# Down projections of a two-layer decoder by 2x2-block products, with block results accumulated in DRAM

## The chip, the cores and the metric

The kernel runs on one core of one Trainium2 chip. A core has five engines with a queue each: PE (matrix products; its weight loads are counted apart as PEld), DVE (vector work), ACT (scalar functions and copies), POOL, and SP, which here only issues transfers. ACT and POOL can issue transfers too. An engine works its queue in order and waits at an instruction until what it needs is done. The time is that of one execution on the device, in microseconds (us); of several runs the median is given.

## The reference

The model is one inference step for 1024 prompt tokens and 8 sample tokens, together T = 1032, with a residual stream of D = 1024 and two layers. Layer 0 mixes tokens by a gated linear recurrence, layer 1 by attention in a window of 128. After each mixer comes the part that is changed here:

```python
def sq_relu_mlp(x, w_up, w_down):
    return jnp.square(jax.nn.relu(x @ w_up)) @ w_down

yp = yp + sq_relu_mlp(rms_norm(yp, norm_mlp_g[layer]), mlp_w_up[layer], mlp_w_down[layer])
ys = ys + sq_relu_mlp(rms_norm(ys, norm_mlp_g[layer]), mlp_w_up[layer], mlp_w_down[layer])
```

The hidden size is 4096: w_up is 1024 x 4096 and w_down 4096 x 1024. Everything is float32.

## The kernel before

Activations lie transposed, as 128 features by the 1032 tokens, so a residual stream is 8 tiles (`x`), a hidden layer 32 (the *k tiles* of the down projection). A float32 factor is split into a high part, rounded to the format that PE takes, and a low part, the rest. A product then takes three passes: high by high, high by low, low by high (L208 and L486). The cast to the high part is ACT's (L150, L370, L376), the subtraction for the low part DVE's (L151, L371, L377).

**Up projection** (`up`, from L497). Its outputs are made in 16 pairs q of two 128-row tiles: he (even) and ho (odd). Each pair, seen as 2x2 blocks with the tokens cut in two halves of 516, is computed with seven block products instead of eight (`BY`, `ORDER`): the factors of a product are sums of blocks. Weight sums S1 to S4 are made by DVE (L462) and split. One product is 24 matmuls of 258 columns (4 k tiles, 3 passes, 2 parts; `product`, L486). Copies by ACT (L519, L524, L527, L534) and adds by DVE (L521, L528, L530, L532) take the results out of PSUM and combine them; then r squared times the squared relu (L537, L538), and ACT issues the store of the tile to `hid` in DRAM (L539).

**Down projection** (`down`, from L566). Here all is done directly: hidden tiles come back from DRAM, loaded by SP (L548) and split (L376, L377). They are taken in groups of 8, 8, 8, 4 and 4. For a group and each of the 8 output tiles, `proj` runs 9 matmuls of 344 columns for each k tile, and DVE adds the three results into the residual tile x, which stays on chip (L591). x is loaded from the buffer `spill` in the first group (L578). The last group goes together with the next norm (`down_steps`, L310). While a group is computed, the next group's tiles are loaded; the first is prepared during the last up pair (`ahead_of_down`).

Weights come through two raw tiles (`raws`, L144), one unit of 128 x 1024 at a time, in the order of one list. Tiles live in pools: W (12 tiles of 128 x 1024) for weights and their sums, A (33 tiles of 128 x 1032) for activations. A pool hands out its tiles in turn, and whoever gets one waits until its last user is done. PSUM is named by banks in turns; in products a block uses G for the result that collects several products, X or Y for those that stand alone. The code gives the operations in program order; a scheduler places them on each engine's queue, with priority for what `tc.high_priority()` encloses and not before the last PSUM copy for what `tc.issue_after(last["copy"])` encloses. After that each queue's order is fixed.

Of the kernel before, what the change touches and what calls it, by code (L numbers as in the profile page):

```python
# [26 lines left out]
HALF = T // 2  # L27
QT = T // 4
# [28 lines left out]
def trunk(ctx: ExitStack, tc: tile.TileContext, I, O):  # L57
# [83 lines left out]
    def fetch(n):  # L141
        while len(raws) < min(n, len(units)):
            raws.append(rp.tile([P, D], F32, tag="R", name=nm("raw")))
            sp.dma_start(raws[-1], units[len(raws) - 1][2])  # L144
# [23 lines left out]
    for layer in range(2):  # L168
        add_units(f"up{layer}", I["w_up"][layer], 2 * NPAIR, lambda j: None)
        add_units(f"dn{layer}", I["w_dn"][layer], 32, lambda j: W)  # L170
# [259 lines left out]
    PROG = [(q, i) for q in (0, 1) for i in (1, 2)] + [(q, i) for i in (3, 7, 6, 5, 4) for q in (0, 1)]  # L430
    PROG += [(q, i) for q in range(2, NPAIR) for i in ORDER]

# [3 lines left out]
    class PairWeights:  # L436
        def __init__(self, layer):
            self.layer = layer
            self.builds = []
            for q in range(NPAIR):  # L440
                names = ["A11", "A12", "+S1", "+S2", "S2", "+S3", "S3", "S1", "+S4", "A22", "S4"]
                if q < 2:
                    names = ["A11", "A12", "+S1", "+S2", "+S3", "+S4", "A22", "S4", "S3", "S2", "S1"]
                self.builds += [(q, n) for n in names]
# [4 lines left out]
        def source(self, q, name):  # L449
            if q not in self.src:  # L450
                n = f"up{self.layer}"
                ensure(index[n, 2 * q + 1])
                x, y = loaded.pop((n, 2 * q)), loaded.pop((n, 2 * q + 1))
                self.src[q] = {"A21": x[:, 0:512], "A11": x[:, 512:1024], "A12": y[:, 0:512], "A22": y[:, 512:1024]}
            src = self.src[q]
            if name not in src:
                x, y, op = SUMS[name]
                x, y = self.source(q, x), self.source(q, y)
                if name in ("S1", "S3"):
                    src[name, 1] = W("ws")  # L460
                src[name] = src[("S1" if name in ("S1", "S2") else "S3"), 1][:, slice(512, 1024) if name in ("S2", "S4") else slice(0, 512)]
# [3 lines left out]
        def build(self, upto):  # L465
            while self.n < min(upto, len(self.builds)):
                q, name = self.builds[self.n]
                if name[0] == "+":
                    self.source(q, name[1:])
                else:  # L470
                    self.ops[q, name] = op_of(self.source(q, name), W, 512)
                self.n += 1

        def take(self, q, name):
            self.build(self.builds.index((q, name)) + 1)
            return self.ops.pop((q, name))

        def look(self, n):
            self.build(self.builds.index((PROG[n][0], BY[PROG[n][1]][0])) + 1 + LOOK)
# [17 lines left out]
    def up(layer, tok, pw, r, hid, after):  # L497
        ops = tok.ops
        st = {}
        for n, (q, i) in enumerate(PROG):  # L500
            w, x = BY[i]
            if n in (1, 3, 5, 7, 9):
# [3 lines left out]
            wt = pw.take(q, w)  # L506
            if i == 1:
                st[q] = {2: DB("X" if q == 1 else "Y"), "g": DB("G"), "e": A("he"), "o": A("ho")}
            z = st[q]
            alone = i in (1, 2, 7) or (i == 3 and q < 2)  # L510
            if alone and i in (3, 7):
                z[i] = DB("Y" if q == 0 else "X")
            d = z["g"] if i in (1, 5, 6) else z[7] if i == 4 else z.get(i, z["g"])
            product(d, alone, wt, ops[x])
            e, o, g = z["e"], z["o"], inner(z["g"])
            e0, e1, o0, o1 = [quarters(t[:, h]) for t in (e, o) for h in (H0, H1)]
            if i == 1:
                with tc.high_priority():
                    last["copy"] = act.copy(e0, g).ins  # L519
            elif i == 2:  # L520
                dve.tensor_tensor(e0, inner(d), e0, ALU.add)  # L521
            elif i == 6:
                with tc.high_priority():
                    last["copy"] = act.copy(o0, g).ins  # L524
            elif i == 5:
                with tc.high_priority():
                    last["copy"] = act.copy(o1, g).ins  # L527
# [5 lines left out]
            elif i == 3:  # L533
                last["copy"] = act.copy(e1, inner(d)).ins  # L534
            ready = {4: [(o, 2 * q + 1)], 3: [] if alone else [(e, 2 * q)], 5: [(e, 2 * q)] if 3 in z else []}
            for t, k in ready.get(i, []):
                dve.scalar_tensor_tensor(t, t, 0.0, r, ALU.min, ALU.mult)  # L537
                act.activation(t, t, AF.Square)  # L538
                act.dma_start(hid[k], t)  # L539
# [750 lines left out]
```

## Time and profile before

| what | us |
|---|---|
| median of 3 runs (2121.7 to 2123.92) | 2121.81 |
| profiled execution | 2123.98 |
| its span | 2122.2 |
| up stage of layer 0, PE without a break (373.60 to 677.00) | 303.40 |
| down stage of layer 0 but its last group (683.66 to 1001.47) | 317.81 |
| up stage of layer 1 (1444.90 to 1748.50) | 303.60 |
| down stage of layer 1 but its last group (1755.20 to 2073.00) | 317.80 |

The profile page gives busy time per engine, the chain of work that ended last, and the costliest groups of instructions by line, with their mean duration and what ended the idle time before them. In a group, "out<-in" names the tiles. "128x516 f32" is 128 partitions by 516 elements. Transfers are listed by the queue that issued them and the median time from issue to landing.

### The profile page before, as it was taken

To read this page: it belongs to the slowest core of one execution; us is meant where nothing else is said; L and a number is where in the kernel's file an instruction comes from. 1 tells how busy PE (TensorE), PEld (TensorE's weight loads), DVE (VectorE), ACT (ScalarE), POOL (GpSimd) and SP (SyncE) were. 2 spreads that over 40 slices of the span, in tenths; PEclk is the share of its full clock that TensorE was granted. 3 is DMA by queue.
4 is the path that set the end of the run, shared out by engine and by line. 5 is a ranking of instruction groups with operands and counts; after the bars stand their busy time and mean duration, and the time that the engine had idled before them with its cause. 6 is when DMAs were issued, how large, how long until landed. Compare 5 with 4: busy or idle time off the path is not lost.

```text
span 2122.2 us, 35371 instructions
## 1 busy us (share of the span) xinstructions
PE 2084.0 (98%) x14518; PEld 2050.3 (97%) x14518; DVE 1193.7 (56%) x2062; ACT 893.8 (42%) x1633; POOL 198.3 (9%) x294
## 2 busy tenths in 40 slices
PE   6999999999999999999999998999999999999999
PEld 5999999999999999999999997999999999999999
DVE  6988547855555432424757878578555545324142
ACT  5486545534444220211447878555434433112010
POOL 4552100000000000000003444000000000000000
PEclk9999999999999999999999999999999999999999
DMA  5102142232234541321232322622323256313112
GB/s 168 50 21 62 51 163 77 99 102 110 90 120 178 202 140 50 120 80 57 94 85 71 96 58 72 230 71 90 110 90 111 100 180 219 139 52 120 50 51 80
DMA packets 84609, 218.05 MB, mean 103 GB/s; under 512 B 15448, under 2 KB 40544, under 8 KB 84448
## 3 DMA queue, kind: packets, MB, share of 16 engines
q1 hardware_dynamic: 64864, 169.29, 24.9%
q10 hardware_dynamic: 19584, 46.51, 5.6%
q8 instruction: 114, 1.87, 0.4%
q14 instruction: 47, 0.39, 0.1%
HBM read 149.83 MB, written 53.24 MB: 96 GB/s over the span
## 4 chain that ended last, share of the span: by engine, by line
PE 91%; DVE 4%; ACT 3%; issue 1%; POOL 1%; DMA 0%; ACTq 0%; SPq 0%; DVEq 0%; POOLq 0%
PE bD L486 31%; PE bP L208 26%; PE bS L208 16%; PE bT L208 8%; PE bP L677 4%; PE bO L805 2%; PE bS L760 1%; PE bT L781 1%; PE bN L623 1%; PE bS L705 1%; DVE xc L1044 1%; DVE t L289 1%; DVE wl L151 0%; DVE hl L236 0%; ACT wh L150 0%
## 5 line engine op out<-in xcount | busy, mean ns | idle before, releaser
L486 PE MATMUL bD<-op,op 128*128 128x258 f32 x5376 | 654.2, 283 | 1.4 <-ACT ho L527 1.4
L486 PEld LDWEIGHTS bD<-op,op 128*128 128x128 f32 x5376 | 648.9, 189 | 6.5 <-ACT ho L527 6.1
L150 ACT CAST wh<-raw 128x1024 fp32r<-128x1024 f32 (+1 forms) x116 | 117.3, 1019 | 429.8 <-PE bP L208 190.3
L208 PE MATMUL bP<-hdl,wh 128*128 128x344 f32 x768 | 191.2, 320 | 0.0
L208 PE MATMUL bP<-hdh,wl 128*128 128x344 f32 x768 | 191.2, 320 | 0.0
L208 PE MATMUL bP<-hdh,wh 128*128 128x344 f32 x768 | 191.0, 320 | 0.0
L151 DVE TENSOR_TENSOR wl<-raw,wh 128x1024 fp32r<-128x1024 f32 (+1 forms) x113 | 135.5, 1202 | 56.8 <-ACT wh L150 51.6
L591 DVE TENSOR_TENSOR x<-bP,x 128x344 f32<-128x344 f32 x96 | 44.9, 509 | 159.7 <-PE bP L208 156.4
L208 PEld LDWEIGHTS bP<-hdh,wl 128*128 128x128 f32 x768 | 134.2, 188 | 0.0
L208 PEld LDWEIGHTS bP<-hdl,wh 128*128 128x128 f32 x768 | 134.1, 188 | 0.0
L208 PEld LDWEIGHTS bP<-hdh,wh 128*128 128x128 f32 x768 | 134.1, 188 | 0.0
L371 DVE TENSOR_TENSOR op<-ws,op 128x512 fp32r<-128x512 f32 x128 | 87.7, 689 | 76.4 <-ACT op L370 76.2
L208 PE MATMUL bS<-hdh,wh 128*128 128x344 f32 x512 | 127.6, 320 | 0.4 <-ACT he L534 0.4
L208 PE MATMUL bS<-hdl,wh 128*128 128x344 f32 x512 | 127.5, 320 | 0.0
L208 PE MATMUL bS<-hdh,wl 128*128 128x344 f32 x512 | 127.4, 320 | 0.0
L377 DVE TENSOR_TENSOR hdl<-hdl,hdh 128x1032 fp32r<-128x1032 f32 x64 | 77.5, 1228 | 63.5 <-ACT hdh L376 63.4
L376 ACT CAST hdh<-hdl 128x1032 fp32r<-128x1032 f32 x64 | 66.4, 1056 | 86.8 <-DMA hdl<-hid 84.6
L370 ACT CAST op<-ws 128x512 fp32r<-128x512 f32 x128 | 78.7, 619 | 50.4 <-PE bD L486 43.8
L371 DVE TENSOR_TENSOR op<-raw,op 128x512 fp32r<-128x512 f32 x96 | 66.1, 691 | 43.1 <-ACT op L370 42.9
L208 PEld LDWEIGHTS bS<-hdh,wh 128*128 128x128 f32 x512 | 89.4, 188 | 0.6 <-ACT he L534 0.6
L208 PEld LDWEIGHTS bS<-hdl,wh 128*128 128x128 f32 x512 | 89.5, 188 | 0.0
L208 PEld LDWEIGHTS bS<-hdh,wl 128*128 128x128 f32 x512 | 89.4, 188 | 0.0
(294 smaller groups left out, 4204.3 us busy)
## 6 DMA issues: line engine op xcount, KB each, us to landing
hdl<-hid SPq DMA_DIRECT2D x64, 516.0 KB, 6.3
raw<-w_up SPq DMA_DIRECT2D x64, 512.0 KB, 3.5
raw<-w_dn SPq DMA_DIRECT2D x64, 512.0 KB, 3.6
hid<-he ACTq DMA_DIRECT2D x32, 516.0 KB, 3.5
hid<-ho ACTq DMA_DIRECT2D x32, 516.0 KB, 2.6
x<-spill SPq DMA_DIRECT2D x24, 516.0 KB, 6.0
spill<-y ACTq DMA_DIRECT2D x48, 172.0 KB, 1.9
raw<-w_in SPq DMA_DIRECT2D x16, 512.0 KB, 3.7
```

The source lines that it names most:

```text
L150: act.copy(r_(hi[:, sl]), raw[:, sl])
L151: eng.tensor_tensor(r_(lo[:, sl]), raw[:, sl], hi[:, sl], ALU.subtract)
L208: pe.matmul(o, lhsT=r_(wt[:, col(k):col(k) + P]), rhs=r_(xt[:, cs(c)]), start=(k == 0 and a == 0), stop=(k == nk - 1 and a == 2))
L289: dve.scalar_tensor_tensor(t, xs[m][:, cs(c)], V(gname, m), r, ALU.mult, ALU.mult)
L370: act.copy(r_(t[:, 0:n]), src)
L371: dve.tensor_tensor(r_(t[:, n:2 * n]), src, t[:, 0:n], ALU.subtract)
L376: act.copy(r_(hi), lo)
L377: dve.tensor_tensor(r_(lo), lo, hi, ALU.subtract)
L486: pe.matmul(d[:, 512 * b:512 * b + QT], lhsT=r_(wt[:, j * P:j * P + P]), rhs=r_(xt[:, QT * b:QT * b + QT]), start=first and j == 0 and a = ...
L591: dve.tensor_tensor(xs[m][:, cs(c)], ps[c], xs[m][:, cs(c)], ALU.add)
L677: pe.matmul(ps[c], lhsT=r_(wt[:, k * P:k * P + P]), rhs=r_(xt[:, cs(c)]), start=(k == 0 and a == 0), stop=(k == M8 - 1 and a == 2))
L805: pe.matmul(o, lhsT=r_(x), rhs=r_(y[:, d]), start=(n == 0), stop=(n == 3 * (2 - first) - 1))
```

## The change

The first 28 of the 32 k tiles of each down projection (14 of 16 pairs, `NSP`) are also computed by seven products of 2x2 blocks. The last four k tiles, in one group with the norm, stay as they were.

- The 14 pairs are cut in five *chunks* (`CHUNKS`) of 3, 3, 3, 3 and 2 pairs. For each chunk there are four output blocks of 2 x 128 rows: 20 blocks per layer. A block is seven products of 18 matmuls of 258 columns (12 in the last chunk, *chunk 4*), in the same loop as the up pairs (`PROG`, `mlp_products`). `PairWeights` makes the weight sums for both; its operations are 384 columns wide (256 in chunk 4) in the down blocks. The weights in DRAM are laid out anew, in 40 units of 768 or 512 columns and 4 of 1024 per layer.
- The right factors are seven sums of quarters of the hidden pair, 516 columns each. They are made once, as an up pair ends (`sums_of`): four DVE operations, and four stores by ACT into `hsum` in DRAM (seven sums, 258 KB each), in place of the two stores of 516 KB. Pairs 14 and 15 are stored in `hid` as before.
- In the down blocks SP loads the sums again (`load`), each chunk's during the chunk before: 8 over the first three blocks, the other 13 (of 21) over the last block, three per product. Four products after a load is issued, the tile is split into high and low by ACT and DVE (`Ahead.split`).
- A block's two results, he and ho, are taken out of PSUM as in the up pairs. They are not added to tiles on chip: POOL issues a transfer for each that adds it to the residual in DRAM (`accum_op=ALU.add`), 80 in all of 516 KB. After a block's accumulates in chunk 4, POOL also issues the loads of the two x tiles (16 in all), and between them the loads of the last four hidden tiles (`last_tile`; 8 in all).

```diff
+CHUNKS = [range(0, 3), range(3, 6), range(6, 9), range(9, 12), range(12, 14)]
+NSP = CHUNKS[-1][-1] + 1
...
+    PROG += [("dn", b, i) for b in range(4 * len(CHUNKS)) for i in ORDER]
...
+    def load(src, n):
+        t = A("tl")
+        sp.dma_start(t[:, n:2 * n], src)
+        return t[:, 0:n], t[:, n:2 * n]
...
+        def fetch(self, c, upto, step):
+            done = 7 * len(CHUNKS[c]) - len(self.left[c])
+            for _ in range(max(0, min(upto - done, len(self.left[c])))):
+                name, p = self.left[c].pop(0)
+                self.raw.append((step, c, name, load(self.sums[p][:, PLACE[name]], HALF)))
+
+        def split(self, step):
+            with tc.issue_after(last["copy"]):
+                while self.raw and self.raw[0][0] <= step - 4:
+                    _, c, name, t = self.raw.pop(0)
+                    self.ops[c][name].append(op_at(*t))
+
+    def sums_of(e, o, to):
+        t = W("ts")
+
+        def put(k, x):
+            act.dma_start(to[:, k * HALF:k * HALF + x.shape[1]], x)
+
+        put(2, o)
+        yield
+        dve.tensor_tensor(t[:, H0], e[:, H1], e[:, H0], ALU.subtract)
+        dve.tensor_tensor(e[:, H1], o[:, H1], e[:, H1], ALU.subtract)
+        dve.tensor_tensor(t[:, H1], o[:, H1], t[:, H0], ALU.subtract)
+        yield
+        put(0, e)
+        put(4, t)
+        dve.tensor_tensor(o[:, H0], o[:, H0], t[:, H1], ALU.subtract)
+        yield
+        put(6, o[:, H0])
...
+        def last_tile(k):
+            lo, hi = A("hdl"), A("hdh")
+            pool.dma_start(lo, hid[layer][k])
+            return hi, lo
...
+            product(d, alone, wt, (tok if up else ahead).ops[x] if up else ahead.ops[q // 4][x])
...
+            if ready and up:
+                t = z[ready]
                 dve.scalar_tensor_tensor(t, t, 0.0, r, ALU.min, ALU.mult)
                 act.activation(t, t, AF.Square)
-                act.dma_start(hid[k], t)
+                if q >= NSP:
+                    act.dma_start(hid[layer][2 * (q - NSP) + (ready == "o")], t)
+            elif ready:
+                pool.dma_start(acc[2 * (q % 4) + (ready == "o")], z[ready], accum_op=ALU.add)
             if i == (4 if 3 in z else 3):
+                if up and q < NSP:
+                    stores.append(sums_of(e, o, hsum[layer][q]))
                 del st[q]
...
+            if up and q == NPAIR - 1:
+                k = ORDER.index(i)
+                ahead.fetch(0, 3 * (k + 1), n)
+                ahead.split(n)
+            elif not up:
+                c, k = q // 4, 7 * (q % 4) + ORDER.index(i)
+                ahead.split(n)
+                if c + 1 < len(CHUNKS):
+                    ahead.fetch(c + 1, 8 * k // 20 if k <= 20 else 8 + len(CHUNKS[c]) * (k - 20), n)
                 else:
+                    if k in (2, 6, 10, 14):
+                        raw.append(last_tile((k - 2) // 4))
+                    if k in (5, 9, 13, 17):
+                        with tc.issue_after(last["copy"]):
+                            hs.append(op_at(*raw.pop()))
+                    if i == 3:
+                        for m in (2 * (q % 4), 2 * (q % 4) + 1):
+                            xs.append(A("x"))
+                            pool.dma_start(xs[m], acc[m])
```

How this moves instructions shows at three places of layer 0. The names in the rows: spill1 is the residual in DRAM, hid0 the hidden tiles, hsum0 the stored sums, raw a raw weight tile, tl a sum, hdl and hdh a hidden tile's low and high part, bD a PSUM bank, op and wh split weights. In brackets stand the counters that a row waits for: DMASW those of transfers issued by POOL, DMAHW of the others. First, before the change, SP's queue in the first group of `down`, where x and the next group's hidden tiles are loaded between weights.

```order
L578 DMA x805_7215<-spill1_2533 128x1032 [waits DMAHW6_49,PE_49]
L548 DMA hdl809_7223<-hid0_2535 128x1032 [waits PE_49]
L144 DMA raw824_7399<-w_dn 128x1024 [waits DMAHW4_49,DMAHW0_49,DVE_49]
L144 DMA raw833_7490<-w_dn 128x1024 [waits DMAHW5_49,DMAHW1_49,DVE_49]
L578 DMA x814_7306<-spill1_2533 128x1032 [waits DMAHW2_49,PE_49]
L548 DMA hdl818_7314<-hid0_2535 128x1032 [waits DMAHW3_49,PE_49]
L578 DMA x823_7397<-spill1_2533 128x1032 [waits PE_49,Pool_49]
L548 DMA hdl827_7405<-hid0_2535 128x1032 [waits PE_49]
```

These rows are gone from SP. The changed kernel's POOL queue in chunk 4; before, POOL issued no transfer. Block 16 has ho1141 and he1140, block 17 ho1163 and he1162.

```order
L613 DMA spill1_2533<-ho1141_10221 128x1032 [waits DMASW2_49,DVE_49]
L613 DMA spill1_2533<-he1140_10220 128x1032 [waits DMASW3_49,Activation_49]
L641 DMA x1158_10355<-spill1_2533 128x1032 [waits DMASW4_49,DMASW3_49,PE_49]
L641 DMA x1159_10357<-spill1_2533 128x1032 [waits DMAHW0_49,DMAHW2_49,DMASW2_49,PE_49]
L571 DMA hdl1171_10435<-hid0_2535 128x1032 [waits DMAHW6_49,DMAHW7_49,DMASW6_49,PE_49]
L613 DMA spill1_2533<-ho1163_10362 128x1032 [waits DMASW7_49,DVE_49]
L613 DMA spill1_2533<-he1162_10361 128x1032 [waits DMASW0_49,Activation_49]
L641 DMA x1178_10495<-spill1_2533 128x1032 [waits DMASW1_49,DMASW0_49,PE_49]
L641 DMA x1179_10497<-spill1_2533 128x1032 [waits DMASW7_49,PE_49]
L571 DMA hdl1185_10519<-hid0_2535 128x1032 [waits DMAHW6_49,PE_49]
```

The loads of x and of the last hidden tiles have moved from SP to POOL and stand behind the accumulates: x1158 waits for both accumulates of its block, and hdl1171 stands behind it.

Second, ACT's queue before, towards the end of `down`, where it only splits weights and hidden tiles.

```order
L150 CAST wh932_8564<-raw923_8473 128x1024 [waits DMAHW3_49,DVE_49,PE_49]
L150 CAST wh940_8653<-raw931_8562 128x1024 [waits DMAHW4_49,DVE_49,PE_49]
L376 CAST hdh895_8124<-hdl894_8123 128x1032 [waits DMAHW7_49,PE_49]
L376 CAST hdh903_8213<-hdl902_8212 128x1032 [waits DMAHW6_49,PE_49]
L376 CAST hdh911_8302<-hdl910_8301 128x1032 [waits DMAHW0_49,PE_49]
L150 CAST wh948_8742<-raw939_8651 128x1024 [waits DMAHW5_49,DVE_49,PE_49]
L376 CAST hdh919_8391<-hdl918_8390 128x1032 [waits DMAHW1_49]
L376 CAST hdh927_8480<-hdl926_8479 128x1032 [waits DMAHW2_49]
```

No row there reads PSUM. ACT's queue in the changed kernel at blocks 17 (he1162) and 18 (he1182, ho1183).

```order
L596 COPY he1162_10361<-bD1161_10360 128x516 [waits PE_49]
L382 CAST hdh1172_10436<-hdl1171_10435 128x1032 [waits DMASW6_49]
L376 CAST op1207_10688<-ws1197_10616 128x256
L376 CAST op1209_10705<-raw1193_10592 128x256 [waits PE_49]
L376 CAST op1210_10708<-ws1205_10670 128x256 [waits DVE_49]
L153 CAST wh1214_10763<-raw1194_10594 128x1024 [waits DMAHW1_49,PE_49]
L596 COPY he1182_10501<-bD1181_10500 128x516
L596 COPY ho1183_10502<-bD1181_10500 128x516 [waits PE_49]
L153 CAST wh1217_10769<-raw1213_10761 128x1024 [waits DMAHW2_49]
L382 CAST hdh1186_10520<-hdl1185_10519 128x1032 [waits DMASW3_49]
L596 COPY ho1183_10502<-bD1181_10500 128x516 [waits PE_49]
```

PSUM copies (L596), which PE waits for, now stand in the same queue behind casts that wait for POOL's loads: hdh1172 ahead of the copies of block 18, hdh1186 ahead of the second copy into ho1183.

Third, SP's queue in the changed kernel in the last block of chunk 1, where the sums of chunk 2 are loaded (L515) beside weights (L147); before, the down stage held the rows of the first place here.

```order
L515 DMA tl945_8481<-hsum0_2537 128x516 [waits DMASW1_49]
L147 DMA raw969_8629<-w_dn 128x768 [waits DMAHW5_49,DMAHW2_49,DVE_49]
L147 DMA raw970_8631<-w_dn 128x768 [waits DMAHW3_49,DMAHW6_49,DVE_49,Activation_49]
L515 DMA tl951_8509<-hsum0_2537 128x516 [waits DMAHW4_49,DMASW3_49]
L515 DMA tl952_8511<-hsum0_2537 128x516 [waits PE_49]
L515 DMA tl953_8513<-hsum0_2537 128x516 [waits PE_49]
L515 DMA tl955_8538<-hsum0_2537 128x516 [waits DMAHW7_49,PE_49]
L515 DMA tl956_8540<-hsum0_2537 128x516 [waits DMAHW0_49,PE_49]
L515 DMA tl957_8542<-hsum0_2537 128x516 [waits DMAHW1_49,PE_49]
L515 DMA tl960_8570<-hsum0_2537 128x516 [waits DMAHW2_49,PE_49]
L515 DMA tl961_8572<-hsum0_2537 128x516 [waits DMAHW3_49,PE_49]
L515 DMA tl962_8574<-hsum0_2537 128x516 [waits DMAHW4_49,DMASW5_49,Activation_49]
```

Ten loads of 258 KB stand nearly without a break, two of them waiting for accumulates (DMASW3, DMASW5) of earlier blocks.

170 lines of the change are left out of this document (75 added, 95 removed).

## Prediction

> **What bounds the kernel now.** I read the shares by engine and the chain first, then busy time by stretch, then the groups of the two MLP stages with their durations, last the DMA issues. The stretches are, in order, layer 0's up and down projections and layer 1's; the columns are length, busy time of PE, PEld, DVE, ACT and POOL (with instruction counts), granted TensorE clock, DMA share and GB/s.
>
> ```profile
> PE 2084.0 (98%) x14518; PEld 2050.3 (97%) x14518; DVE 1193.7 (56%) x2062; ACT 893.8 (42%) x1633; POOL 198.3 (9%) x294
> PE bD L486 31%; PE bP L208 26%; PE bS L208 16%; PE bT L208 8%; PE bP L677 4%; PE bO L805 2%; PE bS L760 1%; PE bT L781 1%; PE bN L623 1%; PE bS L705 1%; DVE xc L1044 1%; DVE t L289 1%; DVE wl L151 0%; DVE hl L236 0%; ACT wh L150 0%
> 373.60:677.00 303.40, 303.37 (x2497) 300.85 (x2495) 177.82 (x249) 128.84 (x200) 0.00 (x0) 1.00 0.33 117
> 683.66:1001.47 317.81, 317.81 (x2019) 317.81 (x2018) 112.16 (x155) 61.17 (x60) 0.00 (x0) 1.00 0.32 110
> 1444.90:1748.50 303.60, 303.56 (x2496) 300.97 (x2495) 177.91 (x249) 128.94 (x201) 0.00 (x0) 1.00 0.33 117
> 1755.20:2073.00 317.80, 317.44 (x2015) 317.15 (x2015) 110.79 (x153) 59.67 (x58) 0.00 (x0) 1.00 0.31 105
> 373.60 303.38 PE bD L486 x2496
> 797.12 11.36 PE bP L208 x72
> ```
>
> PE is 98% busy and carries the chain. In all four stretches it works without a break at full clock, so here the time is the number of matmuls times the spacing of one: 303.38/2496 = 121.5 ns for 258 columns (up), 11.36/72 = 157.8 ns for 344 columns (down; over the stretch 317.81/2016 = 157.6). No other engine is above 59% there, POOL does nothing, DMA stands at a third. A saved matmul is saved time until something else is late.
>
> **The change: what PE saves.** Twenty-eight of the 32 k tiles now go by seven products. Before, they took 28 x 8 x 9 = 2016 matmuls of 344 columns per layer, 317.7 us. After, 16 blocks of 7 x 18 and 4 of 7 x 12, together 2352 matmuls of 258 columns, at 121.5 ns 285.8 us. That is -32.0 us per layer, -63.9 in all. The last four tiles and the norm stay. What remains is what comes late.
>
> **Vector and scalar work.** Durations by form, from layer 0's up stage and (last four rows) its down stage:
>
> ```profile
> L371 DVE TENSOR_TENSOR op<-ws,op 128x512 fp32r<-128x512 f32 x57 | 39.2, 689 | 37.5 <-ACT op L370 37.4
> L370 ACT CAST op<-ws 128x512 fp32r<-128x512 f32 x56 | 34.6, 619 | 22.4 <-PE bD L486 21.9 <-DVE ws L462 0.6
> L528 DVE TENSOR_TENSOR ho<-bD,ho 128x516 f32<-128x516 f32 x15 | 10.4, 694 | 11.5 <-ACT ho L527 11.5
> L527 ACT COPY ho<-bD 128x516 f32<-128x516 f32 x15 | 8.8, 590 | 14.0 <-PE bD L486 14.0
> L371 DVE TENSOR_TENSOR op<-x,op 128x516 fp32r<-128x516 f32 x9 | 5.9, 688 | 0.8 <-ACT op L370 0.8
> ...
> L151 DVE TENSOR_TENSOR wl<-raw,wh 128x1024 fp32r<-128x1024 f32 x32 | 38.9, 1216 | 10.9 <-ACT wh L150 10.8
> L377 DVE TENSOR_TENSOR hdl<-hdl,hdh 128x1032 fp32r<-128x1032 f32 x26 | 31.7, 1229 | 30.9 <-ACT hdh L376 30.7
> L376 ACT CAST hdh<-hdl 128x1032 fp32r<-128x1032 f32 x26 | 27.2, 1056 | 42.7 <-DMA hdl<-hid 41.6 <-PE bT L208 1.1
> L591 DVE TENSOR_TENSOR x<-bP,x 128x344 f32<-128x344 f32 x48 | 21.8, 509 | 79.9 <-PE bP L208 78.4 <-DMA x<-spill 1.5
> ```
>
> Up: a pair is 168 x 121.5 = 20.4 us of PE, with 20.4 x 177.82/303.4 = 12.0 us of DVE. The four sums written out per pair (516 columns, 0.69 each) make it 14.7, so 72%: hidden, nothing on the path.
>
> Down, a block of chunks 0 to 3 is 126 x 121.5 = 15.3 us of PE. DVE has seven splits and four sums of weights of 384 columns (between 509 and 689; by the line through them 0.55 each, 6.1), four adds of block results (2.8) and 5.25 splits of sums (3.6): 12.5 us, 82%. In chunk 4 (10.2 us of PE, 256-column weights, one 1.23 us hidden tile) I get 8.6. ACT is at about 60%. So DVE is nearly full but not the bound on average; bursts decide. Before, the adds of L591 and the splits of L151 had 112 of 318 us, so what covered DVE's peaks was idle time of which a fifth is left.
>
> *Up to down.* The 21 sum tiles of chunk 0 are split from the fifth product of the last pair on, three per product. Over those seven products (3 x 2.92 + 4 x 2.19 = 17.5 us) DVE has 14.5 us of splits beside some 10.3 of other work: 7.3 us too much, against three products (7 to 9 us) between a split and its use. Bounds 0 and 7.3 per layer; since the slack about equals the excess but ACT's copies that PE waits for stand among the same splits, I take the middle, 3.5. Both layers: 7.
>
> *Seams between chunks.* Of the next chunk's 21 tiles, 13 are loaded in the last block and split one block later by the same rule: about 15.3 us of DVE work in 10.9 us of PE, 4.4 too much, with some 9 us of slack. Four seams per layer; bounds 0 and 4.4 each. DVE alone would hide this; the loads (below) make me take 1.25: 10 in all.
>
> **Transfers.** The page's issues, then three rows of layer 0's down stretch alone, where the stores run beside loads:
>
> ```profile
> q1 hardware_dynamic: 64864, 169.29, 24.9%
> q10 hardware_dynamic: 19584, 46.51, 5.6%
> q8 instruction: 114, 1.87, 0.4%
> q14 instruction: 47, 0.39, 0.1%
> hdl<-hid SPq DMA_DIRECT2D x64, 516.0 KB, 6.3
> raw<-w_dn SPq DMA_DIRECT2D x64, 512.0 KB, 3.6
> hid<-he ACTq DMA_DIRECT2D x32, 516.0 KB, 3.5
> hid<-ho ACTq DMA_DIRECT2D x32, 516.0 KB, 2.6
> x<-spill SPq DMA_DIRECT2D x24, 516.0 KB, 6.0
> x<-xT SPq DMA_DIRECT2D x8, 516.0 KB, 8.3
> ...
> x<-spill SPq DMA_DIRECT2D x8, 516.0 KB, 6.5
> hid<-ho ACTq DMA_DIRECT2D x1, 516.0 KB, 8.4
> hid<-he ACTq DMA_DIRECT2D x1, 516.0 KB, 8.3
> ```
>
> No DMA issued by POOL and no accumulating one is in the trace, so the 80 accumulates have no price there. Bounds: 2.6 us (a store of the same 516 KB, nearly alone) and 8.4 us (the same store beside loads). They run beside loads, which speaks for the upper end, but 1.5 to 2 us apart rather than in a burst; I take 6.0, the row of the loads from the same buffer. The Trainium skill's page "DMA: Bandwidth & Descriptors", section "Anatomy of one DMA", has a fit for transfers that GpSimd issues, 2.0 us plus the bytes at 436 GB/s: an estimate of 3.2 us here for accumulate and load alike, by which the chunk-4 term below would come to about 2 and the sum to about 2080. Its section "Issuing engines are not separate DMA queues" speaks against that: all transfers share the same engines, and the trace agrees, with 8.4 against 2.6 us for one store.
>
> The up stage's stores grow from 1032 to 1806 KB per pair, and go out behind ACT's other work: with 1024 KB of weights 142 GB/s, against 117/0.33 = 355 when busy. Hidden; the 98 extra store issues come from ACT, which is 42% busy. In a down block of chunks 0 to 3: two accumulates, 5.25 loads of 258 KB and 768 KB of weights, 3.23 MB in 15.3 us, 211 GB/s. In the last block of a chunk it is 13 loads, 5.28 MB, which is 345 GB/s, the whole rate, and if an accumulate reads its target too 18.4 us instead of 15.3. That is what the 1.25 us per seam is for.
>
> *Chunk 4.* Here a wait is added on PE's path. POOL's queue holds, in order: a block's two accumulates, the two x loads that wait for them, then the load of one of the last hidden tiles, then the next accumulates (order shown above). ACT's cast of that tile stands ahead of the PSUM copies of the block after next. From the end of block 16 to that cast: copy and add 1.3, accumulate 6.0, three issues 0.4, load 6.0 (x<-spill), cast 1.06, copy 0.59, about 15.4 us. PE can go on for block 17 and two products, 10.2 + 2.9 = 13.1: it waits 2.3. The next tile's cast stands ahead of a copy that the last product of block 18 needs, 6 x 1.46 = 8.8 us after block 17's end: it waits 6.6. Per layer 8.9, 18 in all. With 2.6 and a load of 3.6 it is 0.4 per layer; with 8.4 and 8.3 it is 18, 36 in all.
>
> Behind POOL's waiting x loads stand only these. On SP a sum's load can wait for an accumulate that still reads its tile; behind it stand the other sums and the next block's weights, which is in the seams' term. Single waits at block ends, and copies behind casts, are priced by the one of before:
>
> ```profile
> PEld bD L486 <- ACT ho L527: 3.0, 14, 0.9
> ...
> 30.00:34.00 4.00, 1.07 (x2) 0.47 (x2) 2.33 (x4) 1.34 (x3) 0.83 (x1) 0.76 0.37 104
> 34.00:38.00 4.00, 0.00 (x0) 0.00 (x0) 3.28 (x6) 1.94 (x4) 0.00 (x0) 0.50 0.35 100
> 38.00:42.00 4.00, 3.91 (x13) 3.47 (x14) 4.00 (x7) 1.95 (x5) 2.21 (x2) 0.50 0.15 61
> ```
>
> 14 waits of together 3.0 us in 14 pairs: 0.2 us each, for the 40 new blocks 8 if all were new; the same waits cost the up stage only 0.4 of PE in 303.4, so I take 3. In the last rows, from the kernel's start, the clock has fallen to 0.50 while PE stood for some 6 us, and is still there in the next 4 us, with PE busy. The page "TensorE: Matmul & The Clock Gate", section "Why this matters for your kernels", puts the limit at gaps of about 3 us; by that the wait of 6.6 us would cost about 2 us more per layer, 2100 instead of 2096. I leave it out of the sum since the rows show only a longer gap.
>
> **Sum.** 2123.98 (the profiled execution: span 2122.2 and 1.78 around it) - 63.9 + 7 + 10 + 18 + 3 = 2098. That execution is 2.2 above the median of 2121.81, so 2096 against the median, about 1.2% faster.
>
> **Rivals.**
> 1. *All is hidden.* Loads and accumulates at the quiet rows, 2.6 and 3.6, and DVE's bursts inside their slack: only the 3 us and about 1 stay, 2060 to 2072. For it: DMA at a third now, and slacks of 7 to 9 us. Against: DVE 82% full, four full-rate stretches per layer.
> 2. *The accumulates are the bound (slower).* If two of a block run one after the other at the slow 516 KB row, 8.3 each, that is 16.6 us against 15.3 and 10.2 us blocks; he and ho tiles come free that late, and PE keeps their pace: 16 x 1.3 + 4 x 6.4 = 46 per layer, 92 in all, 2150 with nothing else, 2167 with the first two terms. It decides from 64/40 = 1.6 us per block upwards. For it: read and write of the target, and the seams' 345 GB/s. Against: two transfers of these rows overlap (the whole rate is 355 GB/s, 1.5 us per 516 KB).
> 3. *DVE is the bound at seams and in chunk 4.* If splits stand ahead of the adds that free PSUM, the 7.3 and 4.4 are paid whole: 15 + 35 in place of 17, 2129 at the median, no gain. For it: its one fixed order. Against: the adds are issued as the products end.
>
> **How the numbers follow.** A measurement tells about 0.2%, 4.2 us, from no change. Hidden 0.15; my sum, 2075 to 2117 by the bounds of its terms, 0.45; DVE paid whole 0.15, of which a third within 0.2%; slow accumulates 0.25. Faster 0.60 (the first two), same 0.05, slower 0.35. The range 2064 to 2155 leaves out the lowest of rival 1 and the upper half of rival 2, about 2 in 10.
>
> **What would show it.** After: 4704 matmuls of down blocks at 121 ns spacing, up pairs still 20.4 us apart, DVE at 70% and ACT at 53% or so of the span; PE's waits in down blocks on ACT copies, largest in chunk 4 with the chain going through POOL's queue and its x and hidden loads; few waits at seams. Accumulates near 6 us to landing. I am wrong if the up pairs lengthen, if accumulates take over 8 us, or if PE waits every block for a free tile.

## The result: slower by 4%, and the profile after

The changed kernel takes 2208.42 us (median of 4 runs, 2206.69 to 2209.69) against 2122.22 (4 runs): a ratio of 1.0404, 95% interval 1.0386 to 1.0422. The prediction was 2096, range 2064 to 2155: wrong in sign and outside the range. By the spans of the two profiled executions it is 2205.7 against 2122.2, 83.5 us more.

The page of the changed kernel: shares by engine, POOL's DMA queue (q0), the groups of the products (L502; "tl" are down blocks, "op" up pairs) and the transfers.

```profile
span 2205.7 us, 38794 instructions
PE 2061.3 (93%) x15190; PEld 2015.9 (91%) x15190; DVE 1454.1 (66%) x2626; ACT 1097.2 (50%) x2157; POOL 281.2 (13%) x398
q0 software_dynamic: 14976, 54.96, 12.8%
L502 PE MATMUL bD<-tl,op 128*128 128x258 f32 x4704 | 612.3, 293 | 99.5 <-ACT ho L596 47.7
L502 PE MATMUL bD<-op,op 128*128 128x258 f32 x5376 | 654.0, 283 | 4.0 <-ACT ho L596 3.3
tl<-hsum SPq DMA_DIRECT2D x196, 258.0 KB, 7.1
raw<-w_up SPq DMA_DIRECT2D x64, 512.0 KB, 3.9
raw<-w_dn SPq DMA_DIRECT2D x64, 384.0 KB, 5.8
spill<-ho POOLq DMA_DIRECT2D x40, 516.0 KB, 6.0
spill<-he POOLq DMA_DIRECT2D x40, 516.0 KB, 9.6
```

PE did 672 matmuls more and is busy 23 us less: that is the 64 saved, less some 41 of slow clock (below). And it stands idle 99.5 us ahead of down products, nearly always for an ACT copy (44.5 of layer 0's 48.8 us; the rest for DVE adds). The matmuls of the up stage cost what they did. A weight load of 384 KB takes 5.8 us to land where 512 KB took 3.6.

By stretches: chunks 1, 2, 3 of layer 0 (the third row ends at the last block of chunk 3), then that block's end with chunk 4, and the same part of layer 1. The columns are those of the same view before.

```profile
760.00:829.00 69.00, 63.37 (x504) 62.49 (x505) 43.58 (x79) 34.16 (x67) 6.96 (x8) 0.97 0.73 189
829.00:896.00 67.00, 63.20 (x504) 62.32 (x504) 42.69 (x78) 33.31 (x65) 6.92 (x8) 0.98 0.75 194
896.00:958.00 62.00, 55.27 (x438) 54.52 (x438) 35.24 (x68) 27.18 (x56) 5.21 (x6) 0.97 0.64 154
958.00:1037.50 79.50, 54.72 (x365) 52.47 (x366) 35.02 (x60) 28.42 (x51) 12.07 (x18) 0.81 0.62 162
...
2075.60:2156.40 80.80, 56.67 (x366) 54.61 (x367) 34.04 (x59) 27.35 (x50) 12.60 (x18) 0.82 0.60 154
```

No engine is the bound in them: DVE, which I had put at 12.5 us and 82% of a block, has 10.9 us a block and is at 63%. PE loses in two ways: it stands, and the clock is below full. PE's timeline of layer 0 from the first down product (start, length, engine, line, operation; in brackets the gap ahead and what ended it):

```profile
683.59 13.48 PE L502 MATMUL bD<-tl,op 128*128 128x258 f32 x108
...
716.37 40.05 PE L502 MATMUL bD<-tl,op 128*128 128x258 f32 x316 [3.34 <-ACT ho L596]
760.37 63.37 PE L502 MATMUL bD<-tl,op 128*128 128x258 f32 x504 [3.94 <-ACT he L596]
829.00 63.20 PE L502 MATMUL bD<-tl,op 128*128 128x258 f32 x504 [5.26 <-ACT he L596]
896.40 39.90 PE L502 MATMUL bD<-tl,op 128*128 128x258 f32 x313 [4.20 <-ACT he L596]
938.73 15.38 PE L502 MATMUL bD<-tl,op 128*128 128x258 f32 x125 [2.43 <-ACT ho L596]
958.28 13.29 PE L502 MATMUL bD<-tl,op 128*128 128x258 f32 x96 [4.17 <-ACT ho L596]
...
976.47 9.82 PE L502 MATMUL bD<-tl,op 128*128 128x258 f32 x58 [3.34 <-DVE ho L600]
991.31 9.76 PE L502 MATMUL bD<-tl,op 128*128 128x258 f32 x60 [5.02 <-ACT he L596]
...
1022.74 4.89 PE L502 MATMUL bD<-tl,op 128*128 128x258 f32 x24 [11.61 <-ACT ho L596]
```

Inside chunks 1 and 2 it runs 504 matmuls without a gap. The gaps stand at the seams (two products into the next chunk) and all over chunk 4. With the smaller ones, left out here, they come to 4.4 us in chunk 0, 20.0 at seams (the two of the last blocks of chunk 3 among them), 24.4 in chunk 4: 48.8. The stage takes 1037.6 - 683.6 = 354.0, so PE's pieces are 305.2, where 2352 matmuls at 121.5 ns are 285.8: 19.4 us of slow clock. Layer 1 loses the same way: 357.4 us for the stage, 50.4 of gaps and 21.2 of clock.

What do the copies wait for? ACT's waits for transfers in layer 0's down stage (us in total, times, longest), then ACT's timeline at the first seam, SP's ahead of it, SP's waits for accumulates in the whole stage, and two stretches of 5 us at the seam:

```profile
ACT op L376 <- DMA raw<-w_dn: 56.5, 21, 6.7
ACT hdh L382 <- DMA hdl<-hid: 7.2, 1, 7.2
ACT wh L153 <- DMA raw<-w_dn: 4.4, 1, 4.4
ACT ho L596 <- DMA spill<-ho: 2.4, 2, 1.6
ACT tl L382 <- DMA tl<-hsum: 0.7, 1, 0.7
```

```profile
747.60 0.59 ACT L596 COPY ho<-bD 128x516 f32<-128x516 f32 x1 [1.66 <-PE bD L502]
748.08 3.27 ACT L382 CAST tl<-tl 128x516 fp32r<-128x516 f32 x6
757.78 0.51 ACT L376 CAST op<-raw 128x384 fp32r<-128x384 f32 x1 [6.43 <-DMA raw<-w_dn]
758.20 0.58 ACT L596 COPY he<-bD 128x516 f32<-128x516 f32 x1
```

```profile
730.69 7.75 SPq L147 DMA_DIRECT2D raw<-w_dn  x2
738.49 11.92 SPq L515 DMA_DIRECT2D tl<-hsum  x13
750.76 0.33 SPq L147 DMA_DIRECT2D raw<-w_dn  x1
```

```profile
SPq L515 <- DMA spill<-he: 12.0, 3, 4.4
```

```profile
745.00:750.00 5.00, 5.00 (x42) 4.83 (x41) 2.91 (x6) 2.92 (x6) 0.00 (x0) 1.00 1.03 321
750.00:755.00 5.00, 5.00 (x44) 5.00 (x43) 3.15 (x6) 1.35 (x3) 0.86 (x1) 1.00 1.06 397
```

It is the weights. SP stood until 738.1 at a weight load that waited for one of the two raw tiles, then issued the 13 sum loads that had queued up behind it, and only then, at 750.8, the next block's weights. Of the 11.9 us for the 13, SP stood 3.7 at a load whose tile an accumulate (`he`, issued at 738.4) still read; there is one such wait ahead of each of the three seam gaps, 12.0 us together, and 11.3 in layer 1. The cast of the weights began at 757.8; in the 10 us before 755 the DMA engines were full (share 1.03 and 1.06). That cast stands in ACT's fixed order ahead of the copy of the block's result, and PE waits for that. The sums themselves, whose splits I had priced, were late by 0.7 us in all.

### The profile page after: what moved, and what is told of

Read it like the earlier page. It is cut to its first block, busy times and chain, and to the rows that moved or that the text cites. A ratio compares the mean times of both kernels' runs of the same rounds, so it can differ in the third digit from the quotient of the medians.

```text
span 2205.7 us, 38794 instructions
## 1 busy us (share of the span) xinstructions
PE 2061.3 (93%) x15190; PEld 2015.9 (91%) x15190; DVE 1454.1 (66%) x2626; ACT 1097.2 (50%) x2157; POOL 281.2 (13%) x398
## 3 DMA queue, kind: packets, MB, share of 16 engines
q0 software_dynamic: 14976, 54.96, 12.8%
HBM read 172.03 MB, written 117.70 MB: 131 GB/s over the span
## 5 line engine op out<-in xcount | busy, mean ns | idle before, releaser
L502 PE MATMUL bD<-tl,op 128*128 128x258 f32 x4704 | 612.3, 293 | 99.5 <-ACT ho L596 47.7
L502 PEld LDWEIGHTS bD<-tl,op 128*128 128x128 f32 x4704 | 599.6, 199 | 112.0 <-ACT ho L596 56.1
L502 PE MATMUL bD<-op,op 128*128 128x258 f32 x5376 | 654.0, 283 | 4.0 <-ACT ho L596 3.3
L502 PEld LDWEIGHTS bD<-op,op 128*128 128x128 f32 x5376 | 649.3, 189 | 8.5 <-ACT ho L596 6.7
L376 ACT CAST op<-ws 128x512 fp32r<-128x512 f32 (+2 forms) x288 | 155.9, 548 | 157.4 <-PE bD L502 87.8
L376 ACT CAST op<-raw 128x512 fp32r<-128x512 f32 (+2 forms) x216 | 118.2, 549 | 215.1 <-DMA raw<-w_dn 119.1
L377 DVE TENSOR_TENSOR op<-raw,op 128x512 fp32r<-128x512 f32 (+2 forms) x216 | 129.2, 599 | 137.7 <-ACT op L376 137.5
L377 DVE TENSOR_TENSOR op<-ws,op 128x512 fp32r<-128x512 f32 (+2 forms) x288 | 170.7, 598 | 53.5 <-ACT op L376 47.5
L596 ACT COPY ho<-bD 128x516 f32<-128x516 f32 x144 | 84.8, 589 | 200.7 <-PE bD L502 192.8
L383 DVE TENSOR_TENSOR tl<-tl 128x516 fp32r<-128x516 f32 x196 | 128.7, 691 | 60.5 <-ACT tl L382 60.4
L596 ACT COPY he<-bD 128x516 f32<-128x516 f32 x144 | 84.8, 589 | 145.7 <-PE bD L502 145.2
L382 ACT CAST tl<-tl 128x516 fp32r<-128x516 f32 x196 | 114.1, 626 | 2.5 <-DMA tl<-hsum 2.0
L600 DVE TENSOR_TENSOR ho<-bD,ho 128x516 f32<-128x516 f32 x72 | 50.0, 694 | 62.1 <-ACT ho L596 61.0
L153 ACT CAST wh<-raw 128x1024 fp32r<-128x1024 f32 (+1 forms) x60 | 58.8, 990 | 38.4 <-DMA raw<-w_in 11.3
L604 DVE TENSOR_TENSOR ho<-bD,ho 128x516 f32<-128x516 f32 x72 | 49.8, 692 | 38.4 <-PE bD L502 38.3
```

The source lines that it names most:

```text
L153: act.copy(r_(hi[:, sl]), raw[:, sl])
L376: act.copy(r_(t[:, 0:n]), src)
L377: dve.tensor_tensor(r_(t[:, n:2 * n]), src, t[:, 0:n], ALU.subtract)
L382: act.copy(r_(hi), lo)
L383: dve.tensor_tensor(r_(lo), lo, hi, ALU.subtract)
L502: pe.matmul(d[:, 512 * b:512 * b + QT], lhsT=r_(wt[:, j * P:j * P + P]), rhs=r_(xt[:, QT * b:QT * b + QT]), start=first and j == 0 and a = ...
```

## The experiments

Two theories were put against each other. *Late weights*: with two raw tiles a weight load can start only when the block before has used its weights up, and 15.3 us blocks have less cover for it than 20.4 us pairs; whatever lengthens the load stops PE. *Rival 2*: the accumulates are the bound.

**E1, plain stores.**

```diff
-                pool.dma_start(acc[2 * (q % 4) + (ready == "o")], z[ready], accum_op=ALU.add)
+                pool.dma_start(acc[2 * (q % 4) + (ready == "o")], z[ready])
```

> The 80 accumulates become plain stores to the same place (the sums over chunks are left out; same bytes, same queue, same waits). In the changed kernel they took 6.0 and 9.6 us to landing and the time was 2208. Rival 2 (accumulates are the bound): nearly the whole loss goes, about 2208 - 92 = 2116 or less. Theory of late weights (each seam's gap of some 4 us is the weight load that stands behind 13 sum loads on SP): the seams' gaps stay, with the 16 engines a little less busy; only chunk 4, where x loads wait for accumulates, gains some 5 to 8 us per layer: 2190 to 2200.

Measured: 2125.98 us, ratio to the kernel before 1.0018 (1.0009 to 1.0027), 82 us less than the changed kernel. POOL's queue, with the same bytes, now takes

```profile
q0 software_dynamic: 14976, 54.96, 7.2%
...
tl<-hsum SPq DMA_DIRECT2D x196, 258.0 KB, 5.8
raw<-w_dn SPq DMA_DIRECT2D x64, 384.0 KB, 3.9
spill<-ho POOLq DMA_DIRECT2D x40, 516.0 KB, 3.6
spill<-he POOLq DMA_DIRECT2D x40, 516.0 KB, 5.7
```

7.2% of a span of 2124.0 is 153 us of all engines, against 282 us (12.8% of 2205.7): 129 us more for 42.3 MB of accumulates. Of the 153, those 42.3 MB have about 118 by their share of the bytes. By this estimate an accumulating transfer holds the engines 2.1 times as long as a store. The weights land in 3.9 instead of 5.8 us, and ACT's waits for them, counted over the whole run, fall from 171.4 to 117.6. My own expectation, 2190 to 2200, took far too little off, and rival 2's, 2116 or less, came nearer: the accumulates are at work in the seams too. They can act there in two ways, and E1 ends both. The engines are free sooner; and no sum load waits on SP for an accumulate to leave its tile: the 13 sums of a seam are issued in 9.3 us instead of 12.2 (means of the six seams into chunks 1 to 3), and PE's gap behind them is 1.1 us at most instead of 3.9 to 5.3.

**E2, weights on POOL's queue** (chunks 0 to 3).

```diff
-            sp.dma_start(raws[-1][:, 0:src.shape[1]], src)
+            u = units[len(raws) - 1]
+            (pool if u[0][:2] == "dn" and u[1] < 32 else sp).dma_start(raws[-1][:, 0:src.shape[1]], src)
```

> The loads of the down weights of chunks 0 to 3 are issued by POOL instead of SP, so no sum load stands ahead of them and they stand ahead of no sum load. Late weights: the three seam gaps of 3.9 to 5.3 us per layer go, with the clock's slow stretch behind each (some 2 us): 6 x 6 = 36 us less, about 2172; gaps inside chunk 4 stay. Rival 2: no change, 2208, or slower, since the weights then wait behind accumulates. If the 16 engines' rate and not the queue holds the weights (share 1.03 in the 15 us ahead of a seam), the gaps shrink by half at most: 2190.

Measured: 2227.51 us, ratio 1.0489 (1.0474 to 1.0505): 19 us slower than the changed kernel. Free of the sum loads, weights now stand beside and behind accumulates; between 738 and 762 us they take

```profile
raw<-w_dn POOLq DMA_DIRECT2D x2, 384.0 KB, 8.5
```

to land, and in place of gaps at seams alone there is one of 0.3 to 4.0 us in nearly every block. That is rival 2's side of the expectation. So SP's order is not the cause by itself; where the load stands only decides which block pays.

**E3, x loaded after the loop.**

```diff
-                    if i == 3:
-                        for m in (2 * (q % 4), 2 * (q % 4) + 1):
-                            xs.append(A("x"))
-                            pool.dma_start(xs[m], acc[m])
+        for m in range(M8):
+            xs.append(A("x"))
+            pool.dma_start(xs[m], acc[m])
```

> The 16 loads of x are issued by POOL after the last block of chunk 4 instead of between the accumulates, so that a hidden tile's load waits for no accumulate. If the x loads' waits on accumulates carry chunk 4's gap of 11.6 (layer 1: 9.4) us on the last hidden tile: these go, and chunk 4 comes 10 us earlier per layer, but x comes later by one accumulate and load, some 5 us, at the start of the last group: 2190 to 2200. If chunk 4's gaps come from its weights (raw waits of 2 to 5 us per load): no change.

Measured: 2190.59 us, ratio 1.0326 (1.0308 to 1.0344), 18 us less. Part of it is the chain that I had worked out for chunk 4, a hidden tile behind x loads behind accumulates: PE's gap on the last hidden tile falls from 11.6 and 9.4 us to 4.5 and 4.3. It does not go, since ACT still waits 5.9 and 5.7 us for that tile, and a new gap of 6.0 and 4.7 us, on weights, follows. The down stages are only 0.8 and 9.9 us shorter; the rest is gained behind layer 0's.

**E4, three raw tiles**, for one activation tile less.

```diff
-    ap = ctx.enter_context(tc.tile_pool(name="ap", bufs=33))
+    ap = ctx.enter_context(tc.tile_pool(name="ap", bufs=32))
-    rp = ctx.enter_context(tc.tile_pool(name="rp", bufs=2))
+    rp = ctx.enter_context(tc.tile_pool(name="rp", bufs=3))
```

> Three raw weight tiles instead of two, for one activation tile less (32). A weight load then no longer waits until the last sum of the block before has been taken. Late weights: ACT's 56 us per layer of waits for w_dn shrink to under 20, the gaps in the last block of chunk 3 and in chunk 4 that a raw wait ends (2.4 + 4.2 + 3.3 + 5.0 per layer) go and the seams' gaps halve: 45 us less with the clock, about 2165. Rival 2: no change. If the sums' tiles are short, one tile less makes it slower by a few us per seam.

Measured: 2132.63 us, ratio 1.0049 (1.0032 to 1.0067), 76 us less with every accumulate in place. The stretches of chunks 0, 1 and 2 and, last, of chunk 4's larger part:

```profile
683.00:760.00 77.00, 77.00 (x634) 76.36 (x632) 61.87 (x109) 48.55 (x95) 7.21 (x8) 1.00 0.79 227
760.00:822.00 62.00, 61.23 (x500) 60.38 (x500) 42.89 (x77) 33.53 (x65) 7.01 (x8) 1.00 0.77 206
822.00:885.00 63.00, 62.44 (x511) 61.46 (x509) 42.86 (x77) 34.12 (x66) 7.01 (x8) 1.00 0.78 210
...
944.00:1001.50 57.50, 40.09 (x270) 37.97 (x271) 25.33 (x40) 20.50 (x35) 9.75 (x14) 0.85 0.79 216
```

The accumulates still take as long (share of POOL's queue 12.9%), and sum loads wait for them on SP even longer (34.6 us in layer 0 against 12.0), and still the gaps at seams are down to 0.5 to 0.7 us, at full clock; ACT's waits for weights, 171.4 us over the whole run of the changed kernel, are 22.5. Rival 2 as I had put it, blocks that wait for their result tiles, is out. What is left of layer 0's gaps lies in chunk 4.

**E10, one activation tile less, two raw tiles**, the control to E4 (only the first of its two edits).

> The changed kernel with 32 instead of 33 activation tiles and two raw tiles: the price of the tile that the third raw tile displaced. In the run with three raw tiles the up stage of layer 0 began 2.6 us later than in the changed kernel. If that is the tile's doing: 2211 to 2220; if tiles were short in the down stage too: over 2225; if one tile less helps by holding sum loads back: under 2200.

Measured: 2221.82 us, ratio 1.0470 (1.0454 to 1.0485): the tile alone costs 13 us. The third raw tile by itself is worth 2221.82 - 2132.63 = 89 us.

**E6, three raw tiles and plain stores** (E4 and E1).

> Three raw tiles and plain stores in place of accumulates (the sums over chunks are left out). What the accumulates still cost once weights have a third tile. Late weights and the accumulates' use of the 16 engines are one loss seen from two sides (each alone took 76 and 82 us): then together they take hardly more in chunks 0 to 3, and only chunk 4 gains, some 6 us per layer: 2115 to 2125. If they were two separate losses, both would go: about 2208 - 158 = 2050.

Measured: 2103.25 us, ratio 0.9912 (0.9897 to 0.9926). Alone the two took 76 and 82 us, together 105, which is more than I had expected: 53 us are one loss that either cures, and with three raw tiles the accumulates still cost 2132.63 - 2103.25 = 29 us. Here PE has layer 0's chunks 0 to 3 in one piece, up to down included:

```profile
686.60:936.00 249.40, 249.40 (x2046) 246.92 (x2045) 177.82 (x322) 139.80 (x274) 18.11 (x34) 1.00 0.60 205
936.00:992.60 56.60, 42.49 (x311) 39.98 (x309) 27.57 (x45) 22.93 (x40) 7.74 (x15) 0.91 0.71 243
```

249.40/2046 = 121.9 ns, with DVE at 71%: the splits of sums and the adds cost PE nothing.

**E9, half of the accumulates plain** (he plain, ho accumulating; two raw tiles).

```diff
-                pool.dma_start(acc[2 * (q % 4) + (ready == "o")], z[ready], accum_op=ALU.add)
+                pool.dma_start(acc[2 * (q % 4) + (ready == "o")], z[ready], **(dict(accum_op=ALU.add) if ready == "o" else {}))
```

> The changed kernel, with the he half of the accumulates as plain stores (for those rows the sums over chunks are left out). If what an accumulate costs is its time on the 16 engines (twice a plain store's, by the queue's share of 12.8% against 7.2%), half of them leave about half of the 82 us: 2165. If it is the latency of the pair's second accumulate (he: 9.6 us to landing, ho: 6.0) that x loads and tiles wait for, nearly all of the gain comes with he alone: 2130.

Measured: 2164.48 us, ratio 1.0199 (1.0182 to 1.0216), 44 us less: half of 82, as the engines' time has it, so the latency of the later one is not the whole price. But the run does not single out the engines' time: with `he` plain, no sum load on SP waits for an accumulate any more either, the 13 sums of a seam take 10.9 us, and the seam gaps are 2.0 to 2.8 us.

**E5, three raw tiles, hidden tiles loaded by SP.**

```diff
-            pool.dma_start(lo, hid[layer][k])
+            sp.dma_start(lo, hid[layer][k])
```

> Three raw tiles, and the loads of the last hidden tiles issued by SP instead of POOL, so that they stand behind no x load that waits for an accumulate. If the order on POOL's queue is what chunk 4 loses by: ACT's waits for hdl in the run with three raw tiles (3.7 + 5.3 + 4.3 in layer 0) go, and with them PE's gaps of 7.1 and 3.5 and the slow clock behind them: 12 us per layer, about 2109, faster than before. If the accumulates' length alone holds chunk 4, the gap moves to the x loads and little changes: 2130.

Measured: 2121.23 us, ratio 0.9997 (0.9987 to 1.0006): 11 us less than E4, half of what I expected. Of PE's gaps in chunk 4 the one of 7.1 us is 1.8 now, but the last hidden tile is still late (ACT waits 6.4 us for it, PE 5.8).

**E7, three raw tiles, the chunk of two pairs first.**

```diff
-CHUNKS = [range(0, 3), range(3, 6), range(6, 9), range(9, 12), range(12, 14)]
+CHUNKS = [range(0, 2), range(2, 5), range(5, 8), range(8, 11), range(11, 14)]
```

> Three raw tiles, and the chunk of two pairs is the first instead of the last (2, 3, 3, 3, 3). The last chunk's blocks are then 15.3 us of PE instead of 10.2, so each chain of accumulate, x load and hidden load has 5 us more: if that chain is what the end of the down stage loses by, chunk 4's gaps (2.6, 7.1, 3.5 in layer 0) shrink by 5 each, 7 us per layer, about 2118. The first chunk then has 14 instead of 21 sums to split at the end of the up stage, but only 10.2 us per block to load the next: a new gap there of 2 to 5 us if the loads are the limit.

Measured: 2127.9 us, ratio 1.0025 (1.0016 to 1.0035): 5 us less than E4, where I had 15. The end loses less (9.9 us of gaps in the last chunk of layer 0 instead of 17.3); in the first chunk, two products into its third block, there is a new gap of 3.9 us, on weights once more (ACT waits 5.5).

**E8, all three** (E4, E5 and E7).

> All three: three raw tiles, short chunk first, hidden tiles on SP. If the two cures of the end of the stage work on the same wait, about as with either alone, 2105 to 2110. Without any loss but the 3 us and the clock it would be 2062.

Measured: 2116.04 us, ratio 0.9978 (0.9960 to 0.9996): 0.2% ahead of the kernel before, and 6 us above what I had expected.

**E11, E8 with two raw tiles.**

> Short chunk first and hidden tiles on SP, with the two raw tiles of the changed kernel. The cures of the stage's end alone: with three raw tiles they were worth 2132.6 - 2116.0 = 17 us. If weights and the end of the stage are separate losses: 2208 - 17 = 2191. If late weights spoil the end too, less: 2200.

Measured: 2178.58 us, ratio 1.0270 (1.0255 to 1.0285), 30 us less than the changed kernel where I had 17. ACT waits 55.0 us for weights in layer 0 as it did in the changed kernel (56.5): the order of chunks does nothing for them, and the third raw tile, with the activation tile that it displaces, is worth 62 us here.

**E12, E8 with weights split earlier.**

```diff
-    LOOK = 4
+    LOOK = 6
```

> Three raw tiles, short chunk first, hidden tiles on SP, and weights split six operations ahead of their product instead of four (LOOK), so raw tiles come free earlier. If what is left of late weights (15 us of ACT's waits in layer 0, one of 5.8 at the first seam) still stops PE: 5 to 8 us less, about 2110. If the splits themselves crowd out the copies that PE waits for, or weight tiles run short: 2116 to 2125.

Measured: 2115.47 us, ratio 0.9963 (0.9947 to 0.9979): not to be told from E8, and the best that computes everything. Its down stage of layer 0 from the first product to the last group (in an execution of 2111.33 us):

```profile
687.00:995.60 308.60, 295.78 (x2358) 290.51 (x2357) 206.63 (x368) 164.47 (x314) 36.74 (x44) 0.98 0.78 213
```

is 308.6 us against 317.8 before: of the 32 us that PE saves 9 are left.

## Why the prediction was wrong

PE's saving was right. Two steps failed: the term for the seams, put at 10 us for sum loads alone, and the clock, put at nothing; chunk 4's term left out what the seams' had left out too, weights that come late because they have two raw tiles and stand behind the sums. The terms one by one:

- **PE's saving, -63.9: right.** With nothing late, E6 has 121.9 ns per matmul against the 121.5 used. Up pairs hardly lengthened (683.6 - 355.1 = 328.5 us for layer 0's stage against 327.9, and 329.4 against 328.1 in layer 1), so the doubled stores are hidden. For the 28 pairs ACT issues 112 stores instead of 56, so 56 more and not 98.
- **Up to down, 7, from DVE's bursts: size about right by luck, cause wrong.** Chunk 0 has 4.4 and 4.8 us of gaps, but in layer 0 the largest, 3.34, stands behind ACT waits for weights of 2.9 and 3.6 us, and in E6, with DVE at 71%, there is none. Rival 3 falls with it.
- **Seams, 10, put down to sum loads: measured 20.0 and 21.5 us, 41.5.** This is the first step that failed. I followed the sums from load to split and asked only for the rate of the transfers. I priced the weights' load behind them with the sums, as one transfer more, and did not ask when it could begin. It begins when one of two raw tiles comes free, behind what SP has queued by then, and takes 7.0 us from issue to cast at the first seam; the third raw tile (E4) ends the gaps at seams. The wait of a sum's load for an accumulate that still reads its tile was named in the prediction and put into this term, at 1.25 us a seam with all the rest. It is 3.4 to 4.4 us at each of the six seams into chunks 1 to 3. (Three rows of SP's queue ahead of the prediction wait for a POOL transfer, not two: DMASW1, DMASW3 and DMASW5.)
- **The accumulates, 6.0 us each: 6.0 (`ho`) and 9.6 (`he`) measured.** The second lies above my bound of 8.4 and above the 8 us that I had named as a sign of being wrong. Their use of the engines, 2.1 times a store, I had considered in a side sentence for the seams alone (18.4 us instead of 15.3) and priced at 1.25. E1 and E9 show about 1 us per accumulate, 82 for 80 of them. A third raw tile ends 53 of the 82 (E6), so most of it is paid through late weights; how it divides between the engines' time and the tiles that sum loads wait for, no run shows. Blocks that wait for their result tiles, as rival 2 had it, are hardly seen: 2.4 us of ACT's waits in layer 0. Rival 2's number was the nearest (2150 to 2167), for another reason.
- **Chunk 4, 18: measured 24.4 and 24.1, 48.5.** The chain through POOL is there, and E3 and E5 bear it out in part. I had two waits of 2.3 and 6.6 us per layer; the first did not come, the second is 11.6 and 9.4, so 21 us against 18. POOL's timeline in the changed kernel:

```profile
1002.07 1.23 POOL L613 DMA_DIRECT2D spill<-he  x1
1013.25 1.11 POOL L641 DMA_DIRECT2D x<-spill  x2 [9.95 <-issue]
1014.35 0.54 POOL L571 DMA_DIRECT2D hdl<-hid  x1
```

  The x loads came 11.2 us after the accumulate's issue, the hidden tile's cast began 6.8 us after its load was issued, and PE stood 11.61. (An issue on POOL takes 0.54 to 0.87 us, where I had 0.4 for three.) But two further gaps per layer, of 3.3 to 6.3 us, are weights again: ahead of each ACT waits 3.5 to 5.5 us for a weight load. That part the term had left out.
- **The clock, 0: measured 19.4 and 21.2, 40.6.** The other step that failed. I had left it out because the rows of before showed a clock of 0.50 only around a gap of about 6 us. But the row 30.00:34.00 has 0.76 already, behind a gap of 3.58 us. The changed kernel shows it after 4 us:

```profile
755.00:760.00 5.00, 1.43 (x12) 1.22 (x11) 1.67 (x4) 2.22 (x5) 0.86 (x1) 1.00 0.97 270
760.00:765.00 5.00, 4.63 (x26) 4.63 (x27) 5.00 (x10) 3.93 (x8) 0.00 (x0) 0.66 0.72 110
765.00:770.00 5.00, 5.00 (x42) 4.83 (x41) 3.81 (x9) 2.75 (x6) 0.00 (x0) 1.00 0.48 139
```

  After the gap of 3.94 us the clock is 0.66 over 5 us, and the 504 matmuls up to the next gap take 63.37 us, 2.1 more than at 121.5 ns each. Behind the gaps of 3.34, 5.26 and 4.20 us it is 1.7, 2.0 and 1.9, behind that of 2.43 us 0.2; from the last gap of chunk 3 on, 10.6 of layer 0's 19.4 are lost. The Trainium skill's page "TensorE: Matmul & The Clock Gate", section "Why this matters for your kernels", warns of gaps over about 3 us; the trace agrees for these. It is no sharp limit, since in E1 a gap of 2.30 us was followed by 2.6 us at 0.63. I had applied it to one gap per layer and left even that out of the sum. In E4, without the seams' gaps, the same windows have 1.00.
- **Small waits, 3: about 8 measured.** The gaps under 1 us come to 3.7 and 4.3 us in the two down stages; they are counted above, in the stretch in which they lie.
- **Not foreseen: 7.7 us.** Of these 6.4 come between layer 0's down stage and layer 1's up stage, nearly all in the last group, where x loads and the norm run beside late accumulates (PE waits 4.0 us there, at a clock of 0.93 over 1037.5 to 1085), and 1.3 in layer 1's up stage.

The sum of what was measured, for a difference of 83.5 us: -63.9 + 9.2 + 41.5 + 48.5 + 40.6 + 7.7 = 83.6. The bounds of my terms, added up, give about 2062 to 2147 and not the 2075 to 2117 that I had given my sum; the 2208 lies above both.

What stays open: E12 lies 53 us above the 2062 that the saving and the 3 us of small waits would give. In layer 0's down stage 308.6 - 285.8 = 23 us of it are in gaps of 0.4 to 3.4 us in the first chunk, at seams and at the end, and in slower matmuls; some is the missing activation tile (13 us in E10). No run took the rest apart, and none ended the sum loads' waits for accumulates while all accumulates stayed.

## What to carry to other kernels

When a stage becomes faster, ask of every prefetch that it inherits whether the time between a buffer coming free and its next use still covers a load, at the load's new duration: a double buffer that was hidden under 20 us blocks was not under 15 us ones. Price a new transfer not by its own latency alone, but also by the time that it keeps the DMA engines and by how long it holds its tile: a load into that tile waits, and on the same queue everything behind the load. And a gap of PE of some 4 us is paid once more in the clock behind it.

## What the runs showed of the hardware

- An accumulating transfer to DRAM, issued by POOL, kept the DMA engines 2.1 times as long as a plain store of the same bytes (an estimate from the queue's shares: about 247 against 118 us for 42.3 MB), and landed in 6.0 and 9.6 us instead of 3.6 and 5.7 (medians of the two of a block, beside loads). The HBM counters of the two runs are alike, 172.03 MB read and 117.70 written, so they show no read of the target. POOL was busy 0.87 us with issuing each, and 0.53 with a plain store of the same size; ACT and SP took 0.33 for theirs.
- A PE gap of 3.9 us was followed by 5 us at a mean clock of 0.66; gaps of 0.5 to 0.7 us (E4) left it at 1.00. In between it varied: 1.00 behind a gap of 2.43 us (changed kernel, 938.7 to 942), 0.63 behind one of 2.30 (E1, 948.4 to 951).
